# Six instead of three steps of an up projection do their two first-half products early, with the results parked in DRAM

## The chip, the cores and the metric

The kernel runs on one core of one Trainium2 chip. The metric is the device time of one execution in microseconds (us); the time of a kernel is the median of several runs. A difference of under 0.2% (2.9 us here) can't be told from no change.

## What is computed

One decoder layer on 1024 positions of width 1024: two groups of attention heads, an output projection with a residual, and then the part that matters here, a gated MLP with a causal depthwise convolution of width 3 over the positions, and a last norm:

```python
h = rmsnorm(x, ffn_norm_g[l])
u = causal_dwconv(h @ w_up[l], conv_w[l], conv_b[l])   # w_up: 1024 x 5632
gate, val = jnp.split(u, 2, axis=-1)
x = x + (jax.nn.silu(gate) * val) @ w_down[l]          # w_down: 2816 x 1024
return rmsnorm(x, final_norm_g)
```

## The kernel before

Everything is float32, and each product is made of three matmuls on split numbers: an operand `a` is kept as a high part `ah` (a cast by ScalarE, ACT) and a remainder `al = a - ah` (a subtraction by VectorE, DVE, or by GpSimd, POOL), and `mm3` (L158 to L161) adds ah·bh, ah·bl and al·bh in PSUM.

The up projection has 22 steps `j` (`NJ`), one for each block of 128 gate columns with its 128 value columns. A step multiplies a 2 x 2 block of weights (two halves of the input width by gate and value) with a 2 x 2 block of activations (two halves of the width by two halves of the positions) by a scheme with seven products instead of eight. `PORD` is their order: a11, s2, a22, a12, s1, s3, s4. A product is 12 matmuls of 128 x 512. On the weights' side s1 to s4 are sums and differences of the weight tiles (`sums` and `sums2`, four POOL operations for a step); on the side of the activations the operands are `b11`, `b21`, `b22` (blocks as they are) and `t1` to `t4` (sums and differences of blocks), each of four tiles with a high and a low part.

The two products a11 and a12 need only `b11` and `b21`, which belong to the first half of the positions. That half is normed while the output projection of the second half still runs. The other five need the normed second half. Between the output projection and the steps lies a transition, in which DVE norms the second half (L765), forms the differences (L951 to L971) and the low parts (`lo`, L938), 36 differences and low parts and 6 norming operations in all, POOL norms two tiles (L948), and ACT casts the high parts. For the first `NPRE` = 3 steps TensorE (PE) does a11 and a12 ahead, in the transition: `first(j)` and `second(j)`. Their results stay in PSUM or go to a buffer `hold` in SBUF (two buffers, tag `hl`): ACT copies a11 (L932), DVE adds a12 to it (`c11(j)`, L941). In its loop such a step then has five products, a later one seven.

After the products of a step DVE combines them (L1073 to L1090), ACT and DVE do the convolution (`conv`: ACT L1001, four DVE operations at L1003, gate `tg` and value `tv`), ACT the SiLU (L1097), DVE the gating (L1098). After each odd step `combine` (L1047 to L1055) makes the operands of the down projection from two steps and `save` sends seven pieces to DRAM (`td`).

The order on PE, DVE, ACT and POOL is made by the language's scheduler from the program; what stands in the order rows below is its result. The queue of SyncE (SP) alone, which issues nearly all DMAs, keeps the order of the program, and an instruction that waits holds up all behind it. `raws(j)` (L863) loads the two weight tiles of step j (512 KB each) into `wraw`, which has two buffers. `ahead_to` prepares weights four products ahead, so `raws(j)` of an even step stands on SP's queue behind the saves of a pair of steps before it. `NPRE` also sets for how many steps the weights come by the earlier road `w_up` (L129, halves of 512 columns, cast at L140 and subtracted at L143).

Of the kernel before, what the change touches and what calls it, by code (L numbers as in the profile page):

```python
# [13 lines left out]
ALU = mybir.AluOpType  # L14
# [9 lines left out]
NFOX = 4  # L24
DFF = 2816
NJ = DFF // P
NPRE = 3
KN = (4, 3, 3)
NCH = len(KN)
PLAIN = 2 * sum(KN)  # L30
# [38 lines left out]
def layer(ctx, tc, xT, wqk, wv0, wv, wout, wup, wdn, cols, fbias, yT):  # L69
# [144 lines left out]
    x2d = [[dram.tile([P, 512], F32, name=f"x2d{m}_{c}") for c in range(2)] for m in range(KT)]  # L214
    x2f = [[dram.tile([P, 512], F32, name=f"x2f{m}_{c}") for c in range(2)] for m in range(KT)]
    td = [[dram.tile([P, 512], F32, name=f"td{p}_{i}") for i in range(7)] for p in range(NJ // 2)]

    xpool = ExitStack()
    xgp = xpool.enter_context(tc.tile_pool(name="xgp", bufs=1, side="right"))
# [606 lines left out]
    NS = len(steps)  # L826
    st = [dict() for _ in steps]

    def first(j):
        w = w_up[j]  # L830
        st[j]["m1"] = product(w.get(), 0, b11)
        w.ahead(0.5)

    def second(j):
        w = w_up[j]
        st[j]["m2"] = product(w.get(), 512, b21)
        w.ahead(1.0)

    first(0)
    rr = norm_cols(sqs[1], 4)  # L840
    for q in (3, 7):
        act(x2[q, 1], x2[q, 1], AF.Copy, scale=gcol(C_GF, q))
    norm_rows(rr, 4, rbc[:, 512:])
    first(1)
    first(2)

    stream = [(j, n) for j in range(NS) for n in PORD if j >= NPRE or n not in ("a11", "a12")]
    made, tiles, plain = {}, {}, {}
# [74 lines left out]
            produce(pos[0])  # L923
            pos[0] += 1

    hold, m1, ua = {}, {}, {}
    second(0)
    second(1)
    second(2)
    for j in range(2):  # L930
        hold[j] = stg.tile([P, T], F32, name="hold", tag="hl")
        nc.scalar.copy(hold[j][:, :512], st[j]["m1"])  # L932

    def hi(dst, src):
        nc.scalar.copy(dst[0], src)

    def lo(dst, src):
        nc.vector.tensor_tensor(dst[1], src, f32(dst[0]), ALU.subtract)  # L938

    def c11(j):  # L940
        nc.vector.tensor_tensor(hold[j][:, 512:], st[j]["m2"], hold[j][:, :512], ALU.add)  # L941

    x4 = {}
    for k in range(4):
        f12, f22, f11, f21 = x2[k, 1], x2[k + 4, 1], x2[k, 0], x2[k + 4, 0]
        for q in (k, k + 4):
            if q in (3, 7):
                nc.gpsimd.tensor_tensor(x2[q, 1], x2[q, 1], rbc[:, 512:], ALU.mult)  # L948
            else:
                normed(q, 1)  # L950
        nc.vector.tensor_tensor(f11, f12, f11, ALU.subtract)  # L951
        if k:
            lo(t2[k - 1], x4[k - 1])
        if k == 2:
            x4[k] = x2p.tile([P, 512], F32, name="sqa")
        else:
            x4[k] = stg.tile([P, 512], F32, name="t2f", tag="full")
        nc.vector.tensor_tensor(x4[k], f22, f11, ALU.subtract)
        hi(t2[k], x4[k])
        nc.vector.tensor_tensor(f21, x4[k], f21, ALU.subtract)  # L960
        if k < 2:
            ahead_to(k)
        if k:
            hi(t4[k - 1], x2[k + 3, 0])
    c11(0)
    lo(t2[3], x4[3])
    lo(t4[0], x2[4, 0])
    hi(t4[3], x2[7, 0])
    for k in range(4):
        hi(t1[k], x2[k, 0])  # L970
        nc.vector.tensor_tensor(x2[k, 1], x2[k + 4, 1], x2[k, 1], ALU.subtract)  # L971
    for k in range(1, 4):
        lo(t4[k], x2[k + 4, 0])
    ahead_to(2)
    for k in range(4):
        lo(t1[k], x2[k, 0])
    c11(1)
    for k in range(4):
        hi(t3[k], x2[k, 1])
        lo(t3[k], x2[k, 1])  # L980
# [5 lines left out]

    up = ExitStack()
    upp = up.enter_context(tc.tile_pool(name="upp", bufs=1))
    for j in range(NPRE):
        m1[j] = upp.tile([P, 512], F32, name="m1s", bufs=UA)  # L990
        ua[j] = upp.tile([P, T], F32, name="ua", bufs=UA)
        if j < 2:
            nc.scalar.copy(m1[j], hold[j][:, :512])
            nc.scalar.copy(ua[j][:, :512], hold[j][:, 512:])
        else:
            nc.scalar.copy(m1[j], st[j]["m1"])
            nc.vector.tensor_tensor(ua[j][:, :512], st[j]["m2"], m1[j], ALU.add)

    def conv(t, u, us):
        cw = C_CW + 3 * u  # L1000
# [57 lines left out]
    prev = None  # L1058
    for j in range(NJ):
        d = st[j]  # L1060
        for n in PORD:
            if j < NPRE and n in ("a11", "a12"):
                continue
            ahead_to(idx + 4)
            w, o = made[j, n]
            idx += 1
            ps = product(w, o, bmat[n])
            if n == "a11":
                m1[j] = upp.tile([P, 512], F32, name="m1s", bufs=UA)
                nc.scalar.copy(m1[j], ps)  # L1070
            elif n == "s2":
                u2 = upp.tile([P, 512], F32, name="u2")
                tt(u2, ps, m1[j], ALU.add)  # L1073
            elif n == "a22":
                m4 = ps
            elif n == "s1":
                u4 = upp.tile([P, 512], F32, name="u4")
                tt(u4, ps, u2, ALU.add)
                m5 = ps
            elif n == "s3":  # L1080
                u3 = upp.tile([P, 512], F32, name="u3")
                ub = upp.tile([P, T], F32, name="ub")
                tt(u3, ps, u2, ALU.add)
                tt(ub[:, 512:], m5, u3, ALU.add)
                tt(ub[:, :512], u3, m4, ALU.subtract)
            elif n == "a12":
                ua[j] = upp.tile([P, T], F32, name="ua", bufs=UA)
                tt(ua[j][:, :512], ps, m1[j], ALU.add)
            elif n == "s4":
                tt(ua[j][:, 512:], ps, u4, ALU.add)  # L1090
            if j == NJ - 1:
                operands(n, 0, True)
# [202 lines left out]
```

## Time and profile before

| what | value |
|---|---|
| median of 3 runs | 1442.43 us (1439.91 to 1442.75) |
| the profiled execution, its own time | 1441.58 us |
| its span (first to last recorded instruction) | 1439.6 us |
| PE, DVE, POOL, ACT busy, share of the span | 92%, 78%, 60%, 43% |
| transition and up projection | about 704 to 1174 us of the span |

Busy time is a sum over stages with different limits, so it is to be read by stage. A DVE or POOL operation that waits inside the instruction for a resource counts as busy for all of that time. A matmul's recorded length (0.40 us) overlaps the next; the distance of two starts is what one costs.

### The profile page before, as it was taken

What the parts mean: (1) busy time and instruction counts of PE and PEld (TensorE: products, weight loads), DVE (VectorE), ACT (ScalarE), POOL (GpSimd) and SP (SyncE); (2) the same over time, 40 slices, a digit from 0 to 9 for tenths busy, and PEclk for the clock granted to TensorE, in tenths of its full rate; (3) what the DMA queues carried; (4) which work ended last, traced back from release to release, by engine and by line L of the source; (5) the groups of instructions that cost most, each with busy time, mean ns of one, the idle gap of its engine ahead of it and who ended that gap; (6) DMA issues with size and microseconds to landing.
All of it is one profiled execution on the core that took longest, in us unless ns stands there. A gap on an engine that the chain in (4) does not pass through costs nothing.

```text
span 1439.6 us, 19147 instructions
## 1 busy us (share of the span) xinstructions
PE 1317.6 (92%) x6640; PEld 1075.9 (75%) x6640; DVE 1116.7 (78%) x1588; ACT 620.8 (43%) x1128; POOL 859.4 (60%) x730
## 2 busy tenths in 40 slices
PE   7899999999898887889778899999999998999995
PEld 5878878877787765777556688888888865878785
DVE  6246555655676677786899999998888889899987
ACT  5134434444454554353443434443443354344334
POOL 7344454543747573455667788878878763454423
PEclk9999999999999999999889999999999998999997
DMA  5556555545444454547311233333322355554313
GB/s 179 183 161 187 152 154 163 147 147 135 149 121 124 119 159 143 179 147 270 125 44 59 84 106 110 110 110 110 110 97 95 96 176 204 180 171 132 126 36 117
DMA packets 97232, 194.89 MB, mean 135 GB/s; under 512 B 8680, under 2 KB 35688, under 8 KB 97136
## 3 DMA queue, kind: packets, MB, share of 16 engines
q1 hardware_dynamic: 96272, 193.04, 42.6%
q8 instruction: 52, 0.85, 0.3%
q10 hardware_dynamic: 864, 0.64, 0.1%
q14 instruction: 44, 0.36, 0.1%
HBM read 132.79 MB, written 60.85 MB: 135 GB/s over the span
## 4 chain that ended last, share of the span: by engine, by line
PE 50%; DMA 18%; DVE 16%; POOL 7%; issue 6%; SPq 2%; ACT 2%; DVEq 0%; POOLq 0%; ACTq 0%
PE u L161 8%; PE u L160 8%; PE u L159 8%; PE pj L159 5%; PE pj L161 5%; PE pj L160 5%; DMA q<-qkd 4%; DVE fbt L493 3%; DMA vd<-vs 3%; DMA wraw<-in_wqk_dram 2%; DMA wraw<-in_wv_dram 2%; PE tp L505 2%; DMA fbt<-nfd 2%; PE o L526 2%; PE o L525 1%
## 5 line engine op out<-in xcount | busy, mean ns | idle before, releaser
L143 POOL TENSOR_TENSOR wl<-wraw,wh 128x256 fp32r<-128x256 f32 (+2 forms) x134 | 125.3, 952 | 26.9 <-ACT wh L140 21.3
L494 POOL TENSOR_TENSOR w<-w,fbt 128x128 f32<-128x128 f32 (+3 forms) x64 | 90.1, 1417 | 84.4 <-DVE fbt L493 59.9
L904 ACT CAST wh<-s 128x512 fp32r<-128x512 f32 (+1 forms) x136 | 79.8, 591 | 125.7 <-POOL s L879 71.0
L493 DVE TENSOR_TENSOR_SCAN fbt<-fbt 128x128 f32<-128x128 f32 (+3 forms) x64 | 103.5, 1624 | 25.9 <-ACT fbt L480 22.0
L142 POOL TENSOR_SCALAR wh<-wraw 128x256 fp32r<-128x256 f32 (+1 forms) x112 | 55.3, 509 | 108.8 <-DMA wraw<-in_wqk_dram 60.7
L878 POOL TENSOR_TENSOR s<-wraw 128x512 f32<-128x512 f32 (+1 forms) x34 | 55.8, 1641 | 96.0 <-DVE wl L906 53.5
L505 PE MATMUL tp<-ident,w 128*128 128x128 f32 x576 | 94.0, 281 | 19.5 <-DVE pl L514 9.5
L159 PE MATMUL pj<-xh,wh 128*128 128x512 f32 x224 | 103.1, 460 | 5.1 <-DVE yf L293 5.1
L906 POOL TENSOR_TENSOR wl<-wraw,wh 128x512 fp32r<-128x512 f32 x60 | 102.9, 1722 | 0.6 <-ACT wh L904 0.6
L505 PEld LDWEIGHTS tp<-ident,w 128*128 128x128 f32 x576 | 70.7, 144 | 39.1 <-DVE pl L514 12.6
L906 POOL TENSOR_TENSOR wl<-s,wh 128x512 fp32r<-128x512 f32 x48 | 88.5, 1845 | 13.8 <-ACT wh L904 13.4
L514 DVE TENSOR_TENSOR pl<-tp,ph 128x512 fp32r<-128x512 f32 x96 | 64.9, 685 | 40.9 <-ACT ph L513 40.5
L161 PE MATMUL pj<-xh,wl 128*128 128x512 f32 x224 | 91.9, 410 | 0.0
L160 PE MATMUL pj<-xl,wh 128*128 128x512 f32 x224 | 91.3, 407 | 0.0
L485 ACT ACTIVATE w<-w,m 128x128 f32<-128x128 f32 (+3 forms) x64 | 49.7, 776 | 91.1 <-DVE m L475 86.0
L1003 DVE SCALAR_TENSOR_TENSOR tg<-ua,col,tg 128x1023 f32<-128x1023 f32 (+1 forms) x44 | 88.1, 2002 | 0.0
L480 ACT ACTIVATE fbt<-s 128x512 f32<-128x512 f32 (+2 forms) x96 | 47.8, 498 | 83.8 <-PE s L470 39.2
L489 POOL TENSOR_SCALAR w<-w,l 128x128 f32<-128x128 f32 (+3 forms) x64 | 47.6, 748 | 59.9 <-DVE l L488 32.7
L904 ACT CAST wh<-wraw 128x512 fp32r<-128x512 f32 (+1 forms) x96 | 55.1, 589 | 63.1 <-DMA wraw<-in_wdn_dram 25.0
L1003 DVE SCALAR_TENSOR_TENSOR tv<-ub,col,tv 128x1023 f32<-128x1023 f32 (+1 forms) x44 | 76.0, 1727 | 5.7 <-ACT tv L1001 5.6
L513 ACT CAST ph<-tp 128x512 fp32r<-128x512 f32 x96 | 55.7, 590 | 53.1 <-PE o L525 33.4
L885 POOL TENSOR_TENSOR s<-wraw 128x512 f32<-128x512 f32 (+1 forms) x34 | 56.4, 1658 | 35.7 <-DVE wl L906 33.4
(409 smaller groups left out, 4569.4 us busy)
## 6 DMA issues: line engine op xcount, KB each, us to landing
wraw<-in_wup_dram SPq DMA_DIRECT2D x47, 512.0 KB, 3.6
qkd<-hl SPq DMA_DIRECT2D x32, 512.0 KB, 2.9
td<-tg SPq DMA_DIRECT2D x44, 256.0 KB, 2.3
vd<-vs SPq DMA_DIRECT2D x32, 256.0 KB, 4.5
q<-qkd SPq DMA_DIRECT2D x16, 512.0 KB
kh<-qkd SPq DMA_DIRECT2D x32, 256.0 KB, 16.6
kl<-qkd SPq DMA_DIRECT2D x32, 256.0 KB, 17.4
vt<-vd SPq DMA_DIRECT2D x16, 512.0 KB, 17.9
```

What stands on the lines that cost most here:

```text
L143: nc.gpsimd.tensor_tensor(self.lo[:, sl], self.raw[:, sl], f32(self.hi[:, sl]), ALU.subtract)
L159: nc.tensor.matmul(ps, ah, bh, start=start, stop=False)
L160: nc.tensor.matmul(ps, ah, bl, start=False, stop=False)
L161: nc.tensor.matmul(ps, al, bh, start=False, stop=stop)
L493: nc.vector.tensor_tensor_scan(qt[:, rev], qt[:, rev], qt[:, rev], 1.0, ALU.mult, ALU.bypass)
L494: nc.gpsimd.tensor_tensor(w[:, :n], w[:, :n], qt[:, T - n + 1:T + 1], ALU.mult)
L505: nc.tensor.transpose(tp[:, a * 256 + b * P:a * 256 + (b + 1) * P], ws[2 * g + b][:, kb * P:(kb + 1) * P], ident)
L514: nc.vector.tensor_tensor(pl[:, z:], tp[:, z:], f32(ph[:, z:]), ALU.subtract)
L885: nc.gpsimd.tensor_tensor(d["s3"], g[:, :w], v[:, :w], ALU.subtract)
L904: nc.scalar.copy(h[:, o:o + w], src)
L906: eng.tensor_tensor(l[:, o:o + w], src, f32(h[:, o:o + w]), ALU.subtract)
L1003: nc.vector.scalar_tensor_tensor(t[:, s:], us[:, :T - s], col[:, cw + tap:cw + tap + 1], t[:, s:], op0=ALU.mult, op1=ALU.add)
```

## The change

`NPRE` becomes 6. `first(j)` now copies a11 to a `hold` buffer at once, `c11(j)` adds a12 and then writes the whole buffer to a DRAM tile `pd[j]` (512 KB), and `recall(j)` loads it back in two pieces (256 KB each) just before its step: `recall(0)` and `recall(1)` ahead of the loop, `recall(j + 2)` at the start of step j. The early products of steps 2 to 5 stand inside the transition's loop over k. The number of products, matmuls, DVE and POOL operations is the same as before; four ACT copies are gone, and 21 DMAs are added: 6 writes, 12 loads back, and 3 more loads of weights, since the gate tile of an early step is loaded once for its early products and once more for its loop.

```diff
-NPRE = 3
+NPRE = 6
...
+    pd = [dram.tile([P, T], F32, name=f"pd{j}") for j in range(NPRE)]
...
     def first(j):
         w = w_up[j]
-        st[j]["m1"] = product(w.get(), 0, b11)
+        ps = product(w.get(), 0, b11)
         w.ahead(0.5)
+        hold[j] = stg.tile([P, T], F32, name="hold", tag="hl")
+        nc.scalar.copy(hold[j][:, :512], ps)
...
+    def c11(j):
+        nc.vector.tensor_tensor(hold[j][:, 512:], st[j]["m2"], hold[j][:, :512], ALU.add)
+        nc.sync.dma_start(pd[j], hold[j])
...
+    second(0)
     first(1)
-    first(2)
...
-        if k < 2:
-            ahead_to(k)
+        if k < NPRE - 2:
+            c11(k)
+            first(k + 2)
+            second(k + 2)
...
-    c11(0)
...
     hi(t4[3], x2[7, 0])
+    c11(NPRE - 2)
+    ahead_to(0)
+    ahead_to(1)
...
+    c11(NPRE - 1)
     ahead_to(2)
...
+    def recall(j):
+        if j < NPRE:
+            m1[j] = upp.tile([P, 512], F32, name="m1s", bufs=UA)
+            ua[j] = upp.tile([P, T], F32, name="ua", bufs=UA)
+            nc.sync.dma_start(m1[j], pd[j][:, :512])
+            nc.sync.dma_start(ua[j][:, :512], pd[j][:, 512:])
+
+    for j in range(2):
+        recall(j)
...
     for j in range(NJ):
         d = st[j]
+        recall(j + 2)
```

What the scheduler makes of it stands here at three places. The first is PE's order behind the first early product, a11 of step 0: the column sums of the second half (`ones`), and the spreading of the norm's factors over the partitions (`ident,rr`), on which DVE's norming waits. Before:

```order
L748 MATMUL u<-ones,sqa 128x1
L159 MATMUL pj<-b21h_7184,wh 128x512
L160 MATMUL pj<-b21l_7185,wh 128x512
L748 MATMUL u<-ones,sq 128x1
```

and in the changed kernel:

```order
L749 MATMUL u<-ones,sqa 128x1
L749 MATMUL u<-ones,sq 128x1
...
L184 MATMUL u<-ident,rr 128x128 x4
L159 MATMUL u<-b21h_7190,wh 128x512
L160 MATMUL u<-b21l_7191,wh 128x512
```

Before, nine matmuls with `b21` stand among and behind the sums and ahead of the spreading; now they stand behind it. After the spreading the changed PE has eleven early products one behind the other, and only then the first product of step 0's loop (`t2`).

The second place is SP's queue from the third load of `w_up` on. Before, the weights of steps 0 to 3 (L863) follow at once:

```order
L129 DMA wraw<-in_wup_dram 128x1024
L863 DMA wraw<-in_wup_dram 128x1024 x8
L1039 DMA td_0_152<-tg 128x512
```

and in the changed kernel, where L872 is the same `raws` and L846 the write of a parked result:

```order
L129 DMA wraw<-in_wup_dram 128x1024 x2
L846 DMA pd_229<-hold 128x1024
L129 DMA wraw<-in_wup_dram 128x1024
L846 DMA pd_230<-hold 128x1024
L129 DMA wraw<-in_wup_dram 128x1024
L846 DMA pd_231<-hold 128x1024
L846 DMA pd_232<-hold 128x1024
L846 DMA pd_233<-hold 128x1024
L872 DMA wraw<-in_wup_dram 128x1024 x4
L846 DMA pd_234<-hold 128x1024
L998 DMA m1s<-pd_229 128x512
```

The loads of step 0's weights now stand behind five writes of parked results, the fifth of which (`pd_233`) is that of step 4.

The third place is DVE's order late in the transition of the changed kernel, where that step 4's `c11` is the second row:

```order
L941 TENSOR_TENSOR t3l_7655<-x_0_1_7275,t3h_7654 128x512
L845 TENSOR_TENSOR hold<-u,hold 128x512
L941 TENSOR_TENSOR t3l_7657<-x_1_1_7277,t3h_7656 128x512
L941 TENSOR_TENSOR t3l_7659<-x_2_1_7305,t3h_7658 128x512
L941 TENSOR_TENSOR t3l_7661<-x_3_1_7307,t3h_7660 128x512
L941 TENSOR_TENSOR b22l_7663<-x_4_1_7331,b22h_7662 128x512
```

Ahead of this `c11` DVE has 39 operations behind the norm's factors: 6 norming ones, 29 differences and low parts, and 4 earlier `c11`. Before, the place held no `c11` on which a load waits.

## Rows read from the trace of the kernel before

**Rows 1.** The page, part 1: busy time, share of the span, instructions.
```profile
PE 1317.6 (92%) x6640; PEld 1075.9 (75%) x6640; DVE 1116.7 (78%) x1588; ACT 620.8 (43%) x1128; POOL 859.4 (60%) x730
```

**Rows 2.** Busy time of each engine by stretch, granted clock, DMA share.
```profile
core 0: us, PE busy (x) PEld busy (x) DVE busy (x) ACT busy (x) POOL busy (x), PEclk, DMA share, GB/s
723.00:771.00 48.00, 36.19 (x123) 25.01 (x121) 47.66 (x49) 20.45 (x37) 35.80 (x17) 0.85 0.13 41
771.00:842.00 71.00, 66.47 (x275) 52.69 (x276) 63.61 (x60) 29.93 (x42) 53.50 (x33) 0.98 0.28 99
862.00:1174.00 312.00, 312.00 (x1344) 252.94 (x1343) 279.49 (x247) 126.79 (x177) 250.77 (x153) 1.00 0.32 107
```

**Rows 3.** PE in order of time, transition: start, length, instruction, idle before.
```profile
704.11 0.40 PE L159 MATMUL u<-b11h,wh 128*128 128x512 f32 x1
...
720.35 0.63 PE L159 MATMUL pj<-b21h,wh 128*128 128x512 f32 x1
720.78 0.63 PE L160 MATMUL pj<-b21l,wh 128*128 128x512 f32 x1
...
721.63 1.05 PE L184 MATMUL u<-ident,rr 128*128 128x128 f32 x4
...
771.20 0.50 PE L159 MATMUL u<-t2h,wh 128*128 128x512 f32 x1 [1.00 <-DVE u L1073]
```

**Rows 4.** PE in order of time, first products of steps 4 and 6.
```profile
818.69 0.50 PE L159 MATMUL pj<-b11h,wh 128*128 128x512 f32 x1 [0.22 <-ACT wh L904]
...
821.63 0.51 PE L161 MATMUL pj<-b11h,wl 128*128 128x512 f32 x1 [2.21 <-POOL wl L906]
...
825.36 0.63 PE L159 MATMUL pj<-t2h,wh 128*128 128x512 f32 x1
...
861.90 0.40 PE L159 MATMUL u<-b11h,wh 128*128 128x512 f32 x1
...
864.71 0.39 PE L159 MATMUL u<-t2h,wh 128*128 128x512 f32 x1
```

**Rows 5.** DVE in order of time.
```profile
719.92 0.16 DVE L175 TENSOR_TENSOR rr<-rs_s,rs_t 128x4 f32<-128x4 f32 x1
723.34 3.59 DVE L765 SCALAR_TENSOR_TENSOR x<-x,col,rbc 128x512 f32<-128x512 f32 x2 [3.26 <-ACT rbc L757]
...
731.95 0.74 DVE L765 SCALAR_TENSOR_TENSOR x<-x,col,rbc 128x512 f32<-128x512 f32 x1
732.61 0.68 DVE L960 TENSOR_TENSOR x<-t2f,x 128x512 f32<-128x512 f32 x1
...
749.00 2.48 DVE L971 TENSOR_TENSOR x<-x,x 128x512 f32<-128x512 f32 x4
751.41 1.88 DVE L938 TENSOR_TENSOR t4l<-x,t4h 128x512 fp32r<-128x512 f32 x3
...
778.93 1.28 DVE L1003 SCALAR_TENSOR_TENSOR tv<-ub,col,tv 128x1023 f32<-128x1023 f32 x1 [3.47 <-ACT tv L1001]
...
784.61 1.27 DVE L1003 SCALAR_TENSOR_TENSOR tg<-ua,col,tg 128x1022 f32<-128x1022 f32 x1
...
814.77 2.20 DVE L1003 SCALAR_TENSOR_TENSOR tg<-ua,col,tg 128x1022 f32<-128x1022 f32 x1
...
853.08 2.31 DVE L1003 SCALAR_TENSOR_TENSOR tg<-ua,col,tg 128x1022 f32<-128x1022 f32 x1
```

**Rows 6.** POOL in order of time.
```profile
747.93 9.53 POOL L906 TENSOR_TENSOR wl<-s,wh 128x512 fp32r<-128x512 f32 x1 [4.21 <-ACT wh L904]
...
814.60 1.29 POOL L878 TENSOR_TENSOR s<-wraw 128x512 f32<-128x512 f32 x1 [3.23 <-DMA wraw<-in_wup_dram]
```

**Rows 7.** SP's queue in order of time: start and length of its issues.
```profile
810.24 0.32 SPq L1039 DMA_DIRECT2D td<-x  x1
810.66 16.84 SPq L863 DMA_DIRECT2D wraw<-in_wup_dram  x4
```

**Rows 8.** Busy time of each engine while DVE works from the first to the third convolution.
```profile
778.93:808.33 29.40, 28.88 (x124) 23.09 (x123) 29.28 (x27) 13.03 (x17) 22.97 (x13) 1.00 0.24 80
```

**Rows 9.** The page, part 6: DMA issues, KB each, us to landing.
```profile
wraw<-in_wup_dram SPq DMA_DIRECT2D x47, 512.0 KB, 3.6
```

More of the change, by code (lines that the diff above doesn't have):

```diff
@@ L827, in layer @@
     st = [dict() for _ in steps]
+    hold, m1, ua = {}, {}, {}
     def first(j):
         w = w_up[j]
-        st[j]["m1"] = product(w.get(), 0, b11)
+        ps = product(w.get(), 0, b11)
         w.ahead(0.5)
+        hold[j] = stg.tile([P, T], F32, name="hold", tag="hl")
+        nc.scalar.copy(hold[j][:, :512], ps)
     def second(j):
@@ L924, in ahead_to @@
             pos[0] += 1
-    hold, m1, ua = {}, {}, {}
-    second(0)
     second(1)
[L929 to L932, printed above, removed]
     def hi(dst, src):
@@ L938, in lo @@
         nc.vector.tensor_tensor(dst[1], src, f32(dst[0]), ALU.subtract)
-    def c11(j):
-        nc.vector.tensor_tensor(hold[j][:, 512:], st[j]["m2"], hold[j][:, :512], ALU.add)
     x4 = {}
@@ L976, in layer @@
         lo(t1[k], x2[k, 0])
-    c11(1)
     for k in range(4):
@@ L988, in layer @@
     upp = up.enter_context(tc.tile_pool(name="upp", bufs=1))
[L989 to L997, printed above, removed]
+    def recall(j):
[6 more added lines that the diff above has]
+        recall(j)
     def conv(t, u, us):
```

## The prediction

> **What bounds the kernel now.** I began with the page: PE is busy for 92% of the span [rows 1], so what can be gained is where it is not. The table by stretch says where that is: from 862 to 1174 us PE works 312 of 312 us at full clock, and no change ahead of it can shorten this [rows 2]. There a product takes 864.71 - 861.90 = 2.81 us, 0.234 us for a matmul [rows 4]. From the first early product at 704.11 [rows 3] to the start of step 6 at 861.90 [rows 4] PE does 6 x 7 = 42 products, worth 118.0 us, in 157.8. So some 40 us are lost, all before step 6, and I measure the change by when step 6 has its first product (a11) done: 864.71 before.
>
> Who holds PE up there is seen in the other columns. From 723 to 771 DVE is busy 47.66 of 48 us, PE 36.19 at a clock of 0.85 [rows 2]. And DVE is slow by its neighbour: four operations on 128x512 tiles follow each other at (751.41 - 749.00) / 4 = 0.60 us [rows 5], so the 49 of this stretch are worth 49 x 0.60 + 0.4 (six norming ones are 0.06 longer, 0.74 against 0.68 [rows 5]) = 29.8 us. They took 17.9 more, beside 17 POOL operations: 1.05 us for each. A DVE list thus costs **0.60 us an operation and 1.05 us for each POOL operation beside it**. After the transition, from the first convolution to the third, DVE is still busy 29.28 of 29.40 us [rows 8]: in the five-product steps it, not PE, sets the pace.
>
> **The parts of the change.** *The spreading moves ahead of nine matmuls.* The factors are ready at 719.92 + 0.16 = 720.1 and the spreading began at 721.63, with PE in between on `b21` at the half clock of 1.2 GHz (720.78 - 720.35 = 0.43 us a matmul) [rows 3, 5]. It can begin 1.5 us earlier, and with it DVE's norming: 721.8 instead of 723.34.
>
> *Eleven early products on PE.* From 721.1 (spreading done) they need 11 x 2.81 = 30.9 us, and some 2 more until the clock is up: PE is through at 754.0. For that POOL must make the low parts of w_up 2 to 5, eight operations. They have up to 8 us in hand; the long POOL row (9.53 us instead of some 1.3) shows that one may be held off longer [rows 6], which would make 763.5 of the 754.0 at worst, still ahead of the next point.
>
> *The gate in front of step 0.* On SP step 0's weights stand behind `pd_233`, which waits for DVE's 40th operation of the transition, the `c11` of step 4. Ahead of it are 39 operations, and on POOL 2 norming ones and the 8 low parts: 39 x 0.60 + 0.4 + 10 x 1.05 = 34.3 us, so it starts at 721.8 + 34.3 = 756.1 and ends at 756.8. The write and the next load leave 0.4 us later, 757.2 (810.66 - 810.24 [rows 7]). From such a load to POOL's first sum were 814.60 - 810.66 = 3.9 us [rows 6, 7]; bounds for the unknown traffic beside it are 3.6 [rows 9] and twice that, for the parked 512 KB go out just ahead of it. I take 3.9: 761.1. POOL then does s1, the low part of a22, s2, s3 and the low part of s2, 5 x 1.29 = 6.4 us alone (DVE's list is at its end by then): 767.5. PE stands still from 754.0 until two matmuls on the high part and goes on at 767.5, at the half clock: 10 x 0.43 gives 771.8 for the 13th product. Before, the 13th ended at 771.20 + 2.81 = 774.0 [rows 3]. Six products are done earlier, and most of it is spent on the gate: **2.2 us ahead**.
>
> *Steps 0 to 5.* PE has 29 more products, 81.5 us: it would be ready for step 6 at 853.3. But a11 of step 6 waits for weights. On ACT their cast stands behind the SiLU of step 4, on SP their load behind the saves of steps 2 and 3, and both hang on DVE. At step 4 the kernel before has the same place, with the SiLU of step 2 and the saves of steps 0 and 1: the convolution of step 2 ended at 814.77 + 2.20 = 816.97 [rows 5], PE's first matmul waited for the cast and the third for the low part, and a11 was done at 825.36 [rows 4], 8.4 us later. In the changed kernel step 0's last product ends at 771.8 + 4 x 2.81 = 783.0, its last combination 0.7 later, the convolution takes 784.61 + 1.27 - 778.93 = 6.95 [rows 5]: 790.6. From there four more steps at DVE's pace: before, (816.97 - 785.88) / 2 = 15.55 us for a five-product step [rows 5], against 14.05 on PE. So the convolution of step 4 ends at 790.6 + 4 x 15.55 = 852.8 and a11 of step 6 at 852.8 + 8.4 = 861.2. Against 864.71 that is **3.5 us sooner**, and all behind it moves along, since PE has no gap to give it back in.
>
> *What I cost at nothing.* The loads back: 256 KB pieces, issued a step or two before the combination that reads them, with DMA engines at 0.13 to 0.28 [rows 2]. Only that of step 0 has little cover: it leaves behind step 1's loads, near 770, for a use at 771.8; without cover it costs DVE up to 3.6 us [rows 9] once, in which PE goes on. The four ACT copies that are gone: ACT is at 20.45 of 48 us there [rows 2]. The parked writes: `hold` has two buffers, so that the copy of step j waits for the write of j - 2, about 4 us behind its `c11`; all of them are done before ACT needs them by the times above, and if the one of step 5 is late, ACT's casts for step 0 wait until about 755, ahead of 761.1.
>
> **The sum.** 1441.58 - 3.5 = 1438.1 for the profiled execution; the median of the runs stands 0.85 above it (1442.43), which gives 1438.9.
>
> **Rivals.** *PE sets the pace (faster).* If DVE keeps up, step 6 starts at 853.3 and a11 ends at 856.1: 8.6 us sooner, 1433.8. For it speaks that POOL has fewer low parts in a five-product step, 7.5 operations instead of 9.5. Against it, 29.28 of 29.40 us of DVE [rows 8]: already before, it did not keep up.
>
> *It only reorders (no change).* PE was not what bounded these 40 us; DVE's and POOL's operations are the same number, and moving PE's work to where it waits for them gains nothing. In the stretch that gave the pace POOL did 13 operations, 6.5 a step [rows 8], where the changed steps need 7.5: one more at 1.05 makes the pace 16.6 and a11 of step 6 790.6 + 66.4 + 8.4 = 865.4, 0.7 later: 1443.1. What speaks against it is that POOL could slip operations beside DVE's PSUM operations or its waits. The Trainium skill (SBUF — State Buffer, section "SBUF: two separate sides") has a rule that would make this exact: DVE operations with two SBUF inputs and GpSimd ones share an exclusive lock, held for the whole instruction. By it, with durations from the rows, a five-product step has four convolution operations at 1.2 us, a gating one at about 1.2, and 3.5 others at 0.60, with 7.5 x 1.05 of POOL 16.0 us in all, which is 863.0, 1.7 us sooner: 1440.7, still within this rival's chance. The trace agrees in kind: a POOL operation of 9.53 us stood beside back-to-back DVE work [rows 6], though by a lock passed on at each instruction's end it would have waited for one.
>
> *A ring of waits (slower).* New on SP is that `recall(j + 2)` stands ahead of the next weights, and waits for a `ua` buffer (three of them) that DVE's convolution of step j - 1 frees; the weights of step 4 stand behind both the saves and such a recall. By my times they come at 815.8, and with 3.9 + 6.4 us the first product of step 4 can run at 826.1, PE being ready at 825.2. So there is no room: each us that DVE is late comes back to it as late weights, late products and a DVE that stands in front of a low part (`wl`) in its order. With a pace of 18 us a11 of step 6 ends at 871.0: 6.3 later, 1448.7. It decides from (864.71 + 2.9 - 8.4 - 790.6) / 4 = 17.2 us a step; the same loss comes from a gate that opens 6.4 us later. Against it: the loads of steps 2, 3 and 5 have several us in hand.
>
> **How the numbers follow.** The forecast (pace 15 to 16, 1436.7 to 1440.7) gets 0.38, PE's pace 0.17, reordering 0.28, the ring 0.17. Of the forecast's chance I count 0.30 beyond the 2.9 us (0.2%) that a measurement can tell: faster 0.47, same 0.36, slower 0.17. The range goes from a little under PE's pace, 1433.0, to 1446.5, half way from no change to the ring's case: outside lie a few chances in a hundred below and about one in ten above.
>
> **What would show it.** Right: the norming starts near 721.8; eleven early products end near 754; PE then stands still until 766 to 768, with the clock down; step 0's first weight load leaves at about 757, right behind the fifth parked write; convolutions end 15 to 16 us apart; a11 of step 6 ends at 860 to 862 and PE has no gap from there. Wrong, and by which step: a gate far from 757 (the sum of DVE and POOL operations), a pace of 14 or of 17 and more, gaps of PE inside steps 1 to 3, which I have as free, or a gap behind step 6.

## The result and the profile after

The change made the kernel slower: 1453.11 us (median of 4 runs, 1451.89 to 1453.82) against 1442.59 (4 runs of the kernel before, 1439.91 to 1444.29), a ratio of 1.0063 with a 95% interval of 1.0037 to 1.0090. Timed again (e5 below), it was 1.0047 (1.0034 to 1.0061). So it costs 0.5 to 0.6%, some 7 to 9 us. The profiled execution took 1453.13 us with a span of 1450.8.

The first line of the page of the changed kernel, part 1, stands against [rows 1]:

```profile
PE 1315.2 (91%) x6640; PEld 1078.2 (74%) x6640; DVE 1114.6 (77%) x1588; ACT 619.0 (43%) x1124; POOL 846.1 (58%) x730
```

No engine has more instructions, and DVE, POOL, ACT and PE are busy for less time in a longer span: there is more time in which they wait. To see where, one needs a common point in both traces. I take the column sums of the second half, the last thing before the changed code; before and after:

```profile
712.54 0.59 PE L748 MATMUL u<-ones,sqa 128*128 128x1 f32 x2 [4.72 <-POOL sqa L801]
```

```profile
716.74 0.58 PE L749 MATMUL u<-ones,sqa 128*128 128x1 f32 x2 [3.19 <-POOL sqa L802]
```

Up to here both kernels give every engine the same instructions in the same order, and yet the second profile is 4.20 us late. All times of the changed kernel below are its own; to set them beside those of before, take 4.20 off. From the column sums to the end of the span it took 1450.8 - 716.74 = 734.1 us, before 1439.6 - 712.54 = 727.1. These 7.0 us are what the change costs. PE in order of time, from the spreading to step 6 (columns as in [rows 3, 4]):

```profile
724.33 1.11 PE L184 MATMUL u<-ident,rr 128*128 128x128 f32 x4 [1.50 <-DVE rr L175]
...
757.90 0.39 PE L161 MATMUL u<-b21h,wl 128*128 128x512 f32 x1
769.98 0.79 PE L159 MATMUL pj<-t2h,wh 128*128 128x512 f32 x1 [11.69 <-ACT wh L913]
...
771.79 0.80 PE L161 MATMUL pj<-t2h,wl 128*128 128x512 f32 x1 [0.59 <-POOL wl L915]
...
835.21 0.79 PE L159 MATMUL u<-t2h,wh 128*128 128x512 f32 x1 [5.21 <-ACT wh L913]
...
867.08 0.40 PE L159 MATMUL u<-b11h,wh 128*128 128x512 f32 x1
...
870.74 0.79 PE L161 MATMUL u<-b11h,wl 128*128 128x512 f32 x1 [3.03 <-POOL wl L915]
...
875.17 0.63 PE L159 MATMUL u<-t2h,wh 128*128 128x512 f32 x1
```

Three stalls are left: the gate in front of step 0 (11.69 us), one at step 4 (5.21) and one at step 6 (3.03), and behind each the matmuls last 0.79 and 0.63 us instead of 0.40, as they do at the half clock of 1.2 GHz (the granted clock from 769.98 to 777.00 is 0.50). The end of a11 of step 6, 864.71 before [rows 4], is 875.17, or 870.97 in the time of before: 6.3 late. Most of that is lost in the last of the three places: behind the column sums step 6 starts only 1 us later than before (150.3 against 149.4), since the stalls ahead of it have used up the lead of the six products, and its a11 then takes 8.1 us (867.08 to 875.17) instead of 2.8. SP's queue shows what each stall waited for (L846 is the parked write, L872 the weights, L1044 the saves, L999 a reload), at the gate and from 800 us on:

```profile
747.49 13.31 SPq L846 DMA_DIRECT2D pd<-hold  x3
760.90 12.89 SPq L872 DMA_DIRECT2D wraw<-in_wup_dram  x4
```

```profile
801.25 17.83 SPq L1044 DMA_DIRECT2D td<-tg  x3
...
823.70 0.32 SPq L1044 DMA_DIRECT2D td<-x  x1
...
824.58 0.40 SPq L999 DMA_DIRECT2D ua<-pd  x1
825.03 0.90 SPq L872 DMA_DIRECT2D wraw<-in_wup_dram  x2
...
859.50 0.32 SPq L1044 DMA_DIRECT2D td<-x  x1
859.88 0.92 SPq L872 DMA_DIRECT2D wraw<-in_wup_dram  x2
```

The three parked writes take 13 us to leave, since each waits for its step's `c11` on DVE; the last of them is that of step 4, whose `c11` ends at 760.44, and step 0's weights leave right behind it at 760.90. Step 4's leave at 825.03 behind the saves of steps 0 and 1, step 6's at 859.88 behind those of steps 2 and 3. POOL's first sum of each of the three steps ends a wait for just these loads:

```profile
765.57 1.26 POOL L887 TENSOR_TENSOR s<-wraw 128x512 f32<-128x512 f32 x1 [14.70 <-DMA wraw<-in_wup_dram]
...
829.22 1.28 POOL L887 TENSOR_TENSOR s<-wraw 128x512 f32<-128x512 f32 x1 [7.90 <-DMA wraw<-in_wup_dram]
...
863.69 1.33 POOL L887 TENSOR_TENSOR s<-wraw 128x512 f32<-128x512 f32 x1 [4.76 <-DMA wraw<-in_wup_dram]
```

DVE in order of time, with the ends of the convolutions (L1008) of [rows 5] and the gating of step 5 (L1104):

```profile
726.10 3.56 DVE L766 SCALAR_TENSOR_TENSOR x<-x,col,rbc 128x512 f32<-128x512 f32 x2 [1.83 <-ACT rbc L758]
...
759.77 0.67 DVE L845 TENSOR_TENSOR hold<-u,hold 128x512 f32<-128x512 f32 x1
...
770.55 3.43 DVE L915 TENSOR_TENSOR wl<-s,wh 128x512 fp32r<-128x512 f32 x2 [5.29 <-POOL s L894]
779.88 0.69 DVE L1079 TENSOR_TENSOR u<-pj,m1s 128x512 f32<-128x512 f32 x1 [5.91 <-PE pj L161]
...
795.22 2.31 DVE L1008 SCALAR_TENSOR_TENSOR tg<-ua,col,tg 128x1022 f32<-128x1022 f32 x1
...
811.99 2.32 DVE L1008 SCALAR_TENSOR_TENSOR tg<-ua,col,tg 128x1022 f32<-128x1022 f32 x1
...
828.03 1.28 DVE L1008 SCALAR_TENSOR_TENSOR tg<-ua,col,tg 128x1022 f32<-128x1022 f32 x1
...
848.10 2.31 DVE L1008 SCALAR_TENSOR_TENSOR tg<-ua,col,tg 128x1022 f32<-128x1022 f32 x1
...
866.02 2.31 DVE L1008 SCALAR_TENSOR_TENSOR tg<-ua,col,tg 128x1022 f32<-128x1022 f32 x1
...
885.20 2.30 DVE L1104 TENSOR_TENSOR tg<-tg,tv 128x1024 f32<-128x1024 f32 x1 [0.59 <-ACT tg L1103]
```

From DVE's norming to the end of the gating of step 5, busy time by engine (columns as in [rows 2]), before and after:

```profile
723.34:875.64 152.30, 135.97 (x542) 104.66 (x541) 143.47 (x136) 63.99 (x95) 115.66 (x66) 0.94 0.23 78
```

```profile
726.10:887.50 161.40, 140.30 (x553) 111.23 (x552) 138.19 (x136) 62.37 (x91) 105.16 (x66) 0.88 0.36 122
```

This is the most telling pair. Both have 136 DVE operations and 66 of POOL in it. DVE's busy time fell by 5.3 us (the likely reason, not tested by itself, is that POOL works more often while DVE stands still), its idle time rose from 8.8 to 23.2. From the end of this gating to the end of the span are 564.0 us before and 563.3 after: so the loss lies inside this stretch, which is 9.1 us longer and begins 1.4 us sooner behind the column sums (726.10 - 716.74 against 723.34 - 712.54).

### The profile page after: what moved, and what is told of

Its sections match the earlier page's. It is cut to its first block, busy times and chain, and to the rows that moved or that the text cites. A ratio compares the mean times of both kernels' runs of the same rounds, so it can differ in the third digit from the quotient of the medians.

```text
span 1450.8 us, 19197 instructions
## 1 busy us (share of the span) xinstructions
PE 1315.2 (91%) x6640; PEld 1078.2 (74%) x6640; DVE 1114.6 (77%) x1588; ACT 619.0 (43%) x1124; POOL 846.1 (58%) x730
## 4 chain that ended last, share of the span: by engine, by line
PE 50%; DMA 17%; DVE 15%; POOL 8%; issue 7%; SPq 2%; ACT 2%; DVEq 0%; POOLq 0%; ACTq 0%
PE u L161 8%; PE u L160 8%; PE u L159 8%; PE pj L159 5%; PE pj L160 5%; PE pj L161 5%; DMA q<-qkd 3%; DVE fbt L494 3%; DMA vd<-vs 3%; PE tp L506 2%; DMA wraw<-in_wqk_dram 2%; DMA wraw<-in_wv_dram 2%; PE o L527 2%; POOL wl L143 2%; DMA wraw<-in_wup_dram 1%
## 5 line engine op out<-in xcount | busy, mean ns | idle before, releaser
L143 POOL TENSOR_TENSOR wl<-wraw,wh 128x256 fp32r<-128x256 f32 (+2 forms) x140 | 138.8, 1008 | 37.4 <-ACT wh L140 37.1
L887 POOL TENSOR_TENSOR s<-wraw 128x512 f32<-128x512 f32 (+1 forms) x34 | 54.4, 1601 | 115.4 <-DMA wraw<-in_wup_dram 47.6
L142 POOL TENSOR_SCALAR wh<-wraw 128x256 fp32r<-128x256 f32 (+1 forms) x112 | 51.1, 472 | 111.8 <-DMA wraw<-in_wqk_dram 60.1
L915 POOL TENSOR_TENSOR wl<-wraw,wh 128x512 fp32r<-128x512 f32 x54 | 90.8, 1689 | 0.5 <-ACT wh L913 0.5
L1008 DVE SCALAR_TENSOR_TENSOR tg<-ua,col,tg 128x1023 f32<-128x1023 f32 (+1 forms) x44 | 88.9, 2021 | 0.2 <-ACT tg L1006 0.2
L915 DVE TENSOR_TENSOR wl<-s,wh 128x512 fp32r<-128x512 f32 (+1 forms) x88 | 75.2, 862 | 11.8 <-POOL s L894 7.7
L915 POOL TENSOR_TENSOR wl<-s,wh 128x512 fp32r<-128x512 f32 x48 | 79.7, 1662 | 5.7 <-ACT wh L913 5.3
L278 PE MATMUL pj<-wh,xh 128*128 128x256 f32 (+1 forms) x256 | 78.2, 305 | 1.3 <-DVE yf L294 1.3
L913 ACT CAST wh<-wraw 128x512 fp32r<-128x512 f32 (+1 forms) x90 | 51.5, 588 | 65.0 <-DMA wraw<-in_wdn_dram 25.4
```

The source lines that it names most:

```text
L143: nc.gpsimd.tensor_tensor(self.lo[:, sl], self.raw[:, sl], f32(self.hi[:, sl]), ALU.subtract)
L278: nc.tensor.matmul(ps[:, :n], xh[k][:, sl], h, start=(k == 0), stop=False)
L913: nc.scalar.copy(h[:, o:o + w], src)
L915: eng.tensor_tensor(l[:, o:o + w], src, f32(h[:, o:o + w]), ALU.subtract)
L1008: nc.vector.scalar_tensor_tensor(t[:, s:], us[:, :T - s], col[:, cw + tap:cw + tap + 1], t[:, s:], op0=ALU.mult, op1=ALU.add)
```

## The experiments

Two theories. **Queue:** the loss comes from what stands ahead of weight loads on SP (the parked writes at step 0, reloads and saves later). **DVE and POOL:** whatever PE has done early, DVE with POOL beside it needs its time up to step 5, so that the early products buy nothing. All runs in one table; times in us from each run's own profile, ratios to the kernel before on the same chip. "Stretch" is norming to the gating of step 5; "step 6" and "end" count from the column sums.

| run | ratio (95% interval) | stretch | step 6 | end |
|---|---|---|---|---|
| before | 1 | 152.3 | 149.4 | 727.1 |
| changed, first | 1.0063 (1.0037 to 1.0090) | 161.4 | 150.3 | 734.1 |
| e5 changed again | 1.0047 (1.0034 to 1.0061) | 160.9 | 149.1 | 734.1 |
| e1 gate moved | 1.0037 (1.0021 to 1.0054) | 161.6 | 149.9 | 734.5 |
| e2 saves, reloads moved | 1.0036 (1.0021 to 1.0051) | 161.4 | 147.7 | 735.3 |
| e3 both | 1.0012 (0.9997 to 1.0026) | 155.8 | 142.0 | 728.0 |
| e12 gate, reloads moved | 1.0046 (1.0027 to 1.0064) | 160.2 | 148.1 | 734.6 |
| e4 three steps, parked | 1.0006 (0.9987 to 1.0026) | 156.6 | 151.6 | 728.8 |
| e9 before, low parts by DVE | 0.9997 (0.9979 to 1.0016) | 151.5 | 146.5 | 725.6 |
| e10 changed, low parts by DVE | 1.0010 (0.9992 to 1.0028) | 155.8 | 143.2 | 727.7 |
| e11 e3, low parts by DVE | 1.0011 (0.9991 to 1.0030) | 156.0 | 141.3 | 728.8 |
| e17 e1, low parts by DVE | 1.0002 (0.9986 to 1.0019) | 155.7 | 143.4 | 728.9 |
| *less convolution work:* | | | | |
| e7 before | 0.9930 (0.9916 to 0.9944) | 138.3 | 142.4 | 720.7 |
| e6 changed | 0.9984 (0.9969 to 1.0000) | 149.5 | 145.3 | 723.3 |
| e8 e3 | 0.9989 (0.9969 to 1.0009) | 151.4 | 145.0 | 727.0 |
| e15 before, low parts by DVE | 0.9925 (0.9904 to 0.9945) | 136.9 | 140.8 | 717.2 |
| e14 changed, low parts by DVE | 0.9943 (0.9923 to 0.9963) | 145.2 | 138.9 | 721.1 |
| e13 e3, low parts by DVE | 0.9946 (0.9922 to 0.9969) | 145.6 | 139.0 | 721.2 |
| e16 e1, low parts by DVE | 0.9952 (0.9933 to 0.9971) | 140.9 | 137.1 | 715.9 |

### The queue taken apart (e1 to e4, e12)

e1, the gate:

```diff
         if k < NPRE - 2:
+            if k == NPRE - 3:
+                raws(0)
             c11(k)
```

> The changed kernel with one move: the loads of step 0's weights stand on SP's queue ahead of the fourth parked write instead of behind the fifth. Queue theory (the loss comes from what stands ahead of weight loads on SP): the first weight load of step 0 leaves 5 to 9 us earlier than at 760.90, step 0's first product starts at 762 to 765 instead of 769.98, the first convolution ends some 5 us earlier than 797.5; the stall at step 4 stays, since saves and reloads still stand ahead of its weights. Time 1447 to 1449. Rival, DVE sets the pace whatever SP does: POOL's five operations of step 0 now fall beside DVE's list, which ends some 5 us later than 765.3, and the first convolution ends where it did; time 1452 to 1454.

e2, reloads, combinations and saves behind the next weights (e12 has e1 and the reloads' part of it):

```diff
-        recall(j + 2)
...
             ahead_to(idx + 4)
+            if n == "s1":
+                recall(j + 2)
+            if n == "s1" and j in (2, 4):
+                combine(j // 2 - 1, *late)
...
+        elif j < 4:
+            late = (prev, tg)
```

> The changed kernel with the reloads of a step's parked results and the combinations and saves of the first two pairs of steps moved behind the next weight load (a later place in the program, same operations). Queue theory: the weights of step 4 leave before 815 instead of 825.03, those of step 6 before 845 instead of 859.88; PE has no gap at step 4 (5.2 us before) and a11 of step 6 is done 5 to 8 us earlier than 875.2; time 1445 to 1448. Rival, DVE sets the pace whatever SP does: the five-product steps stay at 17 to 18 us from convolution to convolution and a11 of step 6 stays within 2 us of 875.2; time 1451 to 1454.

e3 has both, e4 is `NPRE = 3` in the changed code:

> Both moves together. Queue theory: the two gains add, 9 to 13 us: 1440 to 1444, level with the kernel before or a little under it. Rival, DVE sets the pace: 1450 to 1454. If only the offset that the profile of the changed kernel had ahead of the changed code (4.2 us at the column sums of the second half) is left: 1446.

> The changed code with NPRE = 3: as many early products as before, but their results parked in DRAM. Queue theory: three reloads come when all buffers are free, so nothing waits behind them; 1442 to 1445. Rival, the parking itself costs (DMA traffic, or DRAM tiles that shift the addresses of others and so slow the code ahead of the transition by the 4.2 us seen in the profile of the changed kernel): 1446 to 1449, with the column sums of the second half at 716 to 717 instead of 712.5.

> The version with both moves, less one: the loads of step 0's weights stand ahead of the fourth parked write and the reloads behind the next weights, but combinations and saves stay where the changed kernel has them. If the reloads are what holds the weights: as both moves, 1.000 to 1.002. If the saves are: as the first move alone, 1.003 to 1.005, with the stall of PE at step 4 (5 to 8 us) still there.

Moving the gate opened it as expected (PE went on at 763.24, the column sums of that profile being 1.2 later) and gained next to nothing: the stretch stayed at 161.6. The windows of e1 say why:

```profile
727.28:888.89 161.61, 138.78 (x559) 108.22 (x558) 147.72 (x136) 62.38 (x91) 113.95 (x66) 0.93 0.37 122
```

The same 136 DVE operations were busy for 147.72 us instead of 138.19: POOL's first weights now stand beside DVE's list, and DVE's idle time has become waits inside its instructions. Nor did DVE's first combination come sooner. In e1 it starts 63.4 us behind the column sums, in the changed kernel 63.1 (779.88 - 716.74), for it now waits for step 0's reload, which stands on SP behind the parked write of step 5:

```profile
781.33 0.69 DVE L1081 TENSOR_TENSOR u<-pj,m1s 128x512 f32<-128x512 f32 x1 [3.47 <-DMA ua<-pd]
```

No run moved that reload (in e3 the same wait is 3.11 us), so what it costs is open. PE's lead went into a longer stall at step 4 (8.25 us instead of 5.21). In e2 the weights of step 4 left 10 us earlier, PE's gaps there are short, and a11 of step 6 is done 6.4 us earlier behind the column sums, as the queue theory had it; but the end came no sooner (735.3), and the moved instructions brought waits of their own: DVE waited 2.43 and 3.03 us for saves to free a buffer. The first combination waited for step 0's reload in e2 as well, but comes no later than in the changed kernel, where it waits 5.91 us for PE:

```profile
777.11 0.69 DVE L1082 TENSOR_TENSOR u<-pj,m1s 128x512 f32<-128x512 f32 x1 [5.86 <-DMA m1s<-pd]
```

Both together took 6.1 us off the end (728.0), less than the 9 to 13 expected, and came level with the kernel before. So neither alone is the cause: each is covered by the other, and the gains are not a sum that one could have had by halves. e12 sorts reloads from saves: with the gate and the reloads from step 2 on moved, a stall at step 4 is still there (5.79 us against 8.25 in e1), and the time is no better, so it is above all the saves that hold the weights.

```profile
832.46 0.80 PE L159 MATMUL u<-t2h,wh 128*128 128x512 f32 x1 [5.79 <-ACT wh L913]
```

e4 shows that parking as such costs nothing that these runs can tell; its interval reaches to 1.0026, and its one profile is 4.3 us longer in the stretch and 1.7 at the end, so a small cost isn't ruled out.

But e3 is only level. Its first product of steps 6, 7 and 8, on PE:

```profile
861.70 0.50 PE L159 MATMUL u<-b11h,wh 128*128 128x512 f32 x1 [0.91 <-ACT wh L913]
```

```profile
886.20 0.40 PE L159 MATMUL u<-b11h,wh 128*128 128x512 f32 x1
```

```profile
908.45 0.40 PE L159 MATMUL u<-b11h,wh 128*128 128x512 f32 x1
```

PE comes to step 6 7.4 us ahead of the kernel before (142.0 against 149.4) and then needs 24.5 and 22.2 us for steps that take it 19.5: all of the lead is given back behind step 6. Behind the first of these rows PE stands still for 4.9 us, in five waits of 0.55 to 1.21 us for low parts of the weights, three by POOL and two by DVE. That isn't e3's alone: in all nine profiles with six early steps and the whole computation step 6 takes PE 24 to 29 us.

### The same again, and less for DVE to do (e5 to e8)

> The changed kernel itself, unaltered, timed in more rounds and profiled a second time. Both theories below have nothing to say of it but this: if the 4.2 us that its first profile had ahead of the changed code belong to the kernel, the column sums of the second half start at 716 to 717 us of the span again; if they are chance, anywhere from 712 to 720, as in the four other kernels so far (714.0 to 719.7). Ratio to before 1.004 to 1.007.

The column sums of e5 start at 718.42, in all nineteen profiles anywhere from 712.54 to 720.97, and its end is again 734.1 behind them. So the 4.20 us lie within chance and aren't shown to belong to the change; the 7.0 us came twice.

e6, e7 and e8 leave the second tap out of twelve convolutions, and with it a part of the computation:

```diff
-        for s, tap in ((1, 1), (2, 0)):
+        for s, tap in ((1, 1), (2, 0))[:1 if u < 12 else 2]:
```

> The changed kernel with less work for DVE: the convolutions of steps 0 to 5 leave out the tap two positions back, which takes 12 operations of 1.27 to 2.31 us, 15 to 28 us in all, off DVE between the norming and the convolution of step 5 (that part of the computation is left out). Theory now: DVE's 135 operations between the norming and the end of the fifth convolution bound every version, whatever PE has done early and whatever stands on SP's queue. By it the time falls well below the kernel before, by some 6 to 12 us: 0.992 to 0.996 of it, and step 6 starts 138 to 142 us behind the column sums instead of 150.3. Rival, the queue on SP with its reloads and saves is what makes the steps late: 1.000 to 1.003, since the weights still come behind the saves, and step 6 starts 147 us or more behind the column sums.

> The kernel before with the same 12 operations left out of the convolutions of steps 0 to 5. DVE theory: it too gains, though less than it is relieved of, since with three steps' early products PE becomes the bound soon: 4 to 8 us, 0.994 to 0.997. Rival (PE and the weights set the pace before): under 2 us, 0.999 to 1.000.

> The version with both moves on SP's queue (weights of step 0 ahead of the fourth parked write; reloads, combinations and saves behind the next weights) with the same 12 operations left out. DVE theory: with DVE relieved PE runs at 14 us a step and its early products are worth what they promised: step 6 starts 126 to 134 us behind the column sums instead of 142.0, steps 6 and 7 take 19.5 us each instead of 24.5 and 22.2, and the time is 8 us or more under that of the relieved kernel before: 0.986 to 0.990. Rival, something else than DVE holds the steps (weights, POOL): 0.997 to 1.001 and steps 6 and 7 stay long.

The kernel before gained 10 us (0.993), more than expected, and PE then has no gap from step 3 on: DVE was its bound, as the DVE theory says. The changed kernel gained about as much (9 us against e5), though its 0.9984 and step 6 at 145.3 fell between the numbers of the two theories. But e8 refutes the theory in that form. With the queue rearranged and DVE relieved, the steps did not become faster: step 6 started at 145.0. Something besides DVE's own operations held them.

### Who makes the weights (e9 to e11, e13 to e17)

One line gives the low parts of the weights of steps 0 to 5 to DVE:

```diff
-        eng = nc.vector if j > NJ or n in (LO_UP if j < NJ else LO_FIRST) else nc.gpsimd
+        eng = nc.vector if j > NJ or n in (LO_UP if j < NJ else LO_FIRST) or j < 6 else nc.gpsimd
```

> The kernel before with one change in who does what: in the loop, all low parts of the weights of steps 0 to 5 are made by DVE (24 operations that POOL did: three for each of the steps 0 to 2, five for each of 3 to 5). Theory: DVE and POOL are held up by each other, so that a POOL operation beside DVE's list costs DVE 1.05 us, more than the 0.60 us that DVE needs to do it itself; then the stretch up to step 6 gets shorter by up to 24 x 0.45 = 10.8 us, less what lay beside other work: 0.993 to 0.998. Rival, DVE's own list alone is the bound: 24 x 0.60 = 14 us more: 1.006 to 1.010.

> The changed kernel with the low parts of the weights of steps 0 to 5 made by DVE (18 operations that POOL did). Theory of the pair DVE and POOL: 18 x 0.45 = 8 us less at most, of which the gate and the stall at step 4 let only part through: 1.000 to 1.004, against 1.0047 unaltered. Rival, DVE's own list alone: 1.009 to 1.012.

> The version with both moves on SP's queue, and the low parts of the weights of steps 0 to 5 made by DVE. Theory of the pair: with the queue's stalls gone too, six early steps are worth something at last: 0.992 to 0.997, against 1.0012 without. Rival, DVE's own list alone: 1.006 to 1.009. If nothing but PE and the queue mattered: 1.001.

In e9 neither theory's numbers came: 24 operations changed hands and nothing moved (0.9997). The stretch is nearly all DVE now, 147.15 of 151.53 us:

```profile
728.66:880.19 151.53, 135.39 (x549) 103.71 (x548) 147.15 (x160) 64.47 (x95) 74.12 (x42) 0.97 0.23 79
```

So by an estimate from these two profiles a POOL low part had cost DVE in the steps about what DVE needs for it, (24 x 0.60 + 0.8) / 24 = 0.63 us, not 1.05. e10 gained 0.4% on the changed kernel, as the pair theory had it; that idle DVE time took up the operations is the likely reason. e11 gained nothing on e3, where that theory had 0.992 to 0.997. Of the versions with the whole computation, those that left the 160 to 162 us of the first group came to 155.7 to 156.6, and none of them beats the kernel before with its 152.3.

> Both moves on SP's queue, the 12 convolution operations of steps 0 to 5 left out (that part of the computation is missing), and the low parts of the weights of steps 0 to 5 made by DVE instead of POOL, so that both DVE and POOL are relieved. Theory: the early products are worth nothing because DVE and POOL together (combinations, convolutions, and the making of weights) need 16 to 18 us for a step whatever PE does; with both relieved the five-product steps take 14 to 15.5 us, step 6 starts 127 to 136 us behind the column sums (145.0 with only the convolutions lighter), and the time falls under that of the relieved kernel before (0.993): 0.984 to 0.990. Rival: it is the two buffers for loaded weights, each step's loads waiting for the last step's sums, not the time of the engines: the steps stay at 16 to 17 us, step 6 starts 140 to 145 us behind the column sums, 0.995 to 0.999.

> The changed kernel, queue unaltered, with DVE and POOL relieved in the same two ways. Theory: better than with the convolutions alone left out (0.9984), but the gate and the saves ahead of the weights of steps 4 and 6 stay: step 6 starts 136 to 142 us behind the column sums, 0.990 to 0.995. Rival of the two buffers: no better than 0.9984.

> The kernel before with the same two reliefs, as the measure for the two others. PE is the bound there from step 3 on already with the convolutions alone relieved (no gap, 19.5 us a step), so by both theories little more can come: step 3 starts 80 to 85 us behind the column sums, 0.990 to 0.994.

With DVE and POOL both relieved, and the queue as in the changed kernel, the first product of steps 0 to 5 (e14, PE):

```profile
768.56 0.80 PE L159 MATMUL pj<-t2h,wh 128*128 128x512 f32 x1 [10.88 <-ACT wh L913]
```

```profile
785.21 0.39 PE L159 MATMUL u<-t2h,wh 128*128 128x512 f32 x1
...
799.10 0.40 PE L159 MATMUL u<-t2h,wh 128*128 128x512 f32 x1
...
813.03 0.39 PE L159 MATMUL u<-t2h,wh 128*128 128x512 f32 x1
...
826.96 0.39 PE L159 MATMUL u<-t2h,wh 128*128 128x512 f32 x1
...
840.89 0.39 PE L159 MATMUL pj<-t2h,wh 128*128 128x512 f32 x1
```

Steps 1 to 4 take 13.9 us each, PE's own pace, with the two load buffers as they were: that rival is out, and the 17.7 us from convolution to convolution in the changed kernel were DVE's and POOL's work, and the waits that hang on it. e13 was worse than expected for its own reason: the combination that e2 moved has DVE waiting for saves (1.56 and 3.60 us) in front of a convolution. Yet e14, though it came as expected, is no faster than e15, the relieved kernel before: PE idles 10.88 us at the gate, and step 0 starts at the half clock and takes 16.6 us.

> As e14 (convolutions of steps 0 to 5 lighter by 12 operations, which leaves that part of the computation out; low parts of their weights by DVE), with the loads of step 0's weights ahead of the fourth parked write, and combinations, saves and reloads left where the changed kernel has them. Theory: with DVE and POOL relieved PE is the bound in the five-product steps (14.0 us a step in e14), so now the gate's idle time, and only now, is worth its length: step 6 starts 129 to 134 us behind the column sums instead of 138.9 and the time falls to 0.988 to 0.991, under the relieved kernel before (0.9925). Rival: the saves ahead of the weights of step 4 take it back: a stall of PE of 4 us or more at step 4, step 6 at 137 to 140, 0.993 to 0.996.

> The whole computation, with the loads of step 0's weights ahead of the fourth parked write and the low parts of the weights of steps 0 to 5 by DVE. Theory: DVE with POOL beside it is the floor, which e10 (1.0010) had reached but for its idle time at the gate; moving the gate fills that time with waits again: 1.000 to 1.003. Rival, the gate is worth what PE waits there: 0.995 to 0.998.

e16's time went the rival's way (0.9952; the interval overlaps that of e15, so neither a gain nor a loss is shown). In its profile step 6 starts 3.7 us ahead of e15 and the end is 1.3 us sooner behind the column sums, a difference too small for one profile each. Part of the lead was lost at step 4 (3.7 us of waits, the rival had 4 or more), whose weights still leave behind the saves:

```profile
823.43 0.50 PE L159 MATMUL u<-t2h,wh 128*128 128x512 f32 x1 [2.37 <-ACT wh L913]
...
825.54 0.80 PE L161 MATMUL u<-t2h,wl 128*128 128x512 f32 x1 [1.37 <-DVE wl L915]
```

e17, the whole computation, is level with before, as the theory of the floor had it. **What stays open:** no run had six early steps with every stall gone and no new wait put in, and none had step 0's reload ahead of the last parked write, so whether they would be worth anything with DVE and POOL relieved was not shown. With the computation complete, four ways to free the queue or shift work on top of the change (e3, e10, e11, e17) ended at 1.000 to 1.001.

## Why the prediction was wrong, point by point

*Right, to within a microsecond (4.20 taken off):* the norming at 721.9 (predicted 721.8); the early products' end at 754.1 (754.0); `c11` of step 4 at 755.6 (756.1); step 0's weights at 756.7 (757.2) and POOL's first sum at 761.4 (761.1); the end of PE's idle time, where the low part came, at 767.6 (767.5). The gate was worked out as it came, and in the transition the price of 1.05 us held: 39 operations and 10 of POOL took 33.7 us (726.10 to 759.77), where I had 34.3.

*The first convolution* ended at 793.3, not 790.6. I took its length from the kernel before, 6.95 us with operations of 1.28 and 1.27 us among the four. Here POOL made step 2's weights beside it, three operations took 2.31 and the whole 8.25 (789.28 to 797.53); step 0's last product, too, was 0.9 later than I had it.

*The pace is the term that failed.* I had 15.55 us from one convolution to the next; the four were 16.78, 15.00, 21.10 and 17.92, mean 17.70. That is 8.6 of the 9.8 us by which a11 of step 6 came later than the forecast's 861.2; the first convolution is 2.7 of them, and from the convolution of step 4 to a11 it took 6.8 us instead of 8.4. DVE's own work was about as I had it: in the four it was busy for 64.27 of 70.80 us, 16.1 a step. The rest is idle time, most of it (3.7 us) in the third, which holds the stall at step 4. The second is short because POOL, waiting 7.90 us for step 4's weights, was busy for only 5.9 us in it, and for 16.5 in the third. So the step "four more steps at DVE's pace" failed in taking the weights as always there.

I had written the cause down as a rival: weights of step 4 behind the saves and a reload, "no room", the loss returning to DVE. I gave it 0.17, because I had set its border on an average pace (17.2 us) and asked whether the average would pass it. By my own times that place needed no slow pace: it was 0.9 us short already (826.1 against 825.2), and the first convolution alone came 2.7 later still. Its case was a pace of 18 with a11 of step 6 done at 871.0; measured were 17.7 and 870.97. Of its two parts the saves did it (801.25 to 824.02 on SP). The reloads held the queue too: that of step 3 stood from 785.50 to 797.59, until the convolution of step 0 had freed its buffer at 797.53, but POOL waited only 0.44 us for the weights behind it, and with the reloads from step 2 on moved the stall at step 4 stayed (e12). The range's upper end was meant half way from no change to this rival's case, which by the numbers there is 1445.6 and not 1446.5; the measured time is beyond both.

The Trainium skill (SBUF — State Buffer, section "SBUF: two separate sides") has DVE operations with two SBUF inputs and GpSimd ones that read SBUF exclude each other for a whole instruction, which had given 16.0 us a step. The trace agrees in size: DVE was busy for 16.1 us a step, with 7 operations of POOL a step, and an operation that grows from 1.27 to 2.31 us beside POOL fits it too.

*The second thing that failed is the sentence that all behind step 6 moves along, since PE has no gap to give it back in.* In e3 PE reached step 6 7.4 us ahead and gave all of it back in steps 6 and 7. PE without a gap in the old trace only meant that the weights and operands were ready by then; come earlier, it waits for DVE and POOL. So with the stalls undone it is the rival "only reorders" that is left, at 1.000 to 1.001.

*Hidden at no cost that shows* were the reloads and the buffers of the writes in the changed kernel, as I had it; where the gate was moved, the reload of step 0, the one with "little cover", cost DVE 3.1 and 3.5 us of waiting (e3, e1). *What I did not count:* while PE stood at the gate, DVE ran out of work. The 5.29 and 5.91 us in the rows above are most of the 14.4 us by which its idle time grew, and DVE was what had bound this stretch. That this idle time is itself the loss is not shown: in e1 it was 9.3 us less, and the stretch stayed as long, the time having gone into longer operations. My sum followed PE and the queue through the gate, and asked of DVE only when `c11` was done.

## What to carry to other kernels

Work moved ahead on one engine pays only if that engine ends the stretch; follow the lead to its end and ask who must be done there, instead of stopping at the first point where the engine has no gap. Where loads stand in order behind waits, as on SP here, a place that is already a microsecond short in one's own sum deserves more than 0.17. When two stalls cover each other, undoing one shows nothing: undo both before calling either innocent.

## What the runs showed of the hardware

Two profiles of the same instructions reached the same point 4.20 us apart. The first step of it is one wait of DVE for a write to DRAM to free a buffer, 1.03 us before and 2.69 after:

```profile
596.74 0.69 DVE L652 TENSOR_TENSOR t<-pj,rbc 128x512 f32<-128x512 f32 x1 [1.03 <-DMA x2d<-t]
```

```profile
598.26 0.69 DVE L653 TENSOR_TENSOR t<-pj,rbc 128x512 f32<-128x512 f32 x1 [2.69 <-DMA x2d<-t]
```

PE, which waited with it, then had a granted clock of 0.63 from 600 to 605 us against 0.94, and came out 2.5 us later against the other profile than it went in (593.39 against 593.65 ahead of it, 603.90 against 601.69 behind). From 635 to 640 us the clock was 0.78 against 1.00, and another 1.6 us were gone. The profile from which I predicted was the earliest of the nineteen at the column sums, so some 4 us either way of a forecast for one profile here is chance.
